# A two-layer diffusion backbone on one core: the MLP's down projection as seven products of quarter blocks instead of eight

## The chip, the cores and the metric

The kernel runs on one core of a Trainium2 chip. The metric is the time of one execution on the device in microseconds (us), from the first to the last instruction with what lies around them. TensorE (PE in the profile) multiplies matrices, VectorE (DVE) and ScalarE (ACT) work elementwise, GpSimd (POOL) does little here, and SyncE (SP) issues DMA transfers. Each engine works through its own list of instructions in a fixed order, and semaphores hold an instruction back until its inputs are there.

## The reference

Two layers over 512 latent tokens `x` and 256 context tokens `h`, width 1024, MLP width 4096, everything in float32. Cut to what matters:

```python
for l in range(2):
    last = l == 1
    sh1, sc1, g1, sh2, sc2, g2 = split(silu(c) @ w_ada[l] + b_ada[l])        # and the same of c_ctx
    ox, oc = token_mix(modulate(rmsnorm(x), sh1, sc1), modulate(rmsnorm(h), csh1, csc1), ...)
    x = x + g1 * ox
    x = x + g2 * (square(relu(modulate(rmsnorm(x), sh2, sc2) @ w_ff1[l])) @ w_ff2[l])
    if not last:
        h = h + cg1 * oc
        h = h + cg2 * (square(relu(modulate(rmsnorm(h), csh2, csc2) @ w_ff1[l])) @ w_ff2[l])
return rmsnorm(x, norm_final)
```

So layer 0 runs its MLP on 768 tokens and layer 1 on 512. `w_ff1` is 1024x4096 and `w_ff2` 4096x1024 in each layer.

## The kernel before

Features lie on the 128 partitions and tokens along the free axis. Float32 accuracy comes from split operands: every operand of a product is kept as a high part (a copy rounded to fp32r) and a low part (the rest), and a product of two blocks is three matmuls, high·high, high·low and low·high (`mm3`, recorded at L150). For a unit of weights (128x1024, 512 KB) SyncE loads the raw block, ACT writes the high part (`hi`, L158) and DVE subtracts it for the low part (`lo`, L167). Activations are split by the same two helpers.

`layer_ff` does the MLP in four chunks of 1024 hidden units. A chunk has two phases. FF1, the up projection: 8 tiles `A` of 128 units, each 8 blocks of `w_ff1` by all tokens (a 512-wide and, in layer 0, a 256-wide matmul for each of the three products). `evac` squares the rectified tile (ACT L1224, DVE L1225) and splits it into an `act` tile. FF2, the down projection: `residual_tasks` makes 8 tiles `res` of 128 outputs from the 8 `act` tiles, and `gate_update` (DVE L1137) adds each, times a gate, to the residual `x`.

In the last chunk the last two output tiles (`TAIL1`) take the token groups (0 to 255, 256 to 511, and in layer 0 512 to 767) one after the other, and the norm of one finished group is strewn among the tiles of the next: squares of `x` are summed (`stat_push`, L432), a product with ones (`ssum`) adds them over partitions, `rstd` (nv, nq, L442 to L446) makes the scale, and `norm_h` (hn at L459, h at L462 and L463) makes the split input of the next layer, whose first products are `rk`. At the very end `fin` (L498) scales the output instead.

`emit` walks the list of tasks in order and puts weight splits ahead of their use: 3 slots for split units (`N_W`), 2 for raw ones (`N_R`). The modulation vectors of layer 1 are not made by matmul but by DVE, as inner products of rows of `w_adaT` (`rows`, `dot`, L390), merged into layer 0's MLP as background work, with 3 slots for those rows. The last part of layer 0's own modulation is eight products on PE (`ada`) with rows of `w_ada` from the same 3 slots; they are merged into the first seven tasks of layer 0's MLP.

PSUM, where products land, has 8 banks of 512 float32 columns; the MLP uses three tiles of two banks and two of one.

## Time and profile before

| | us |
|---|---|
| median of 3 runs | 1603.75 (1602.11 to 1604.69) |
| profiled execution, span from first to last instruction | 1602.4 |
| PE busy in it | 1561.8 (97%) |
| DVE busy | 908.3 (57%) |
| ACT busy | 616.6 (38%) |

The profiled execution has the span of 1602.4 us; what lies around a span is not listed for it, and its span stands within the range of the three runs. A busy share of PE near 100% means that matmuls follow each other without a gap, and what another engine does then is hidden unless a matmul waits for it.

### The profile page before, as it was taken

Reading aid. Unit: us, or ns where it says so; the run is one execution under the profiler, and the core shown is the slowest. Engines: PE = TensorE matmul, PEld = TensorE weight load, DVE = VectorE, ACT = ScalarE, POOL = GpSimd, SP = SyncE. Lnnn points to the kernel's source line nnn. Section 1 sums busy time; section 2 is a strip of 40 time slices with the busy share of each in tenths; the row PEclk is TensorE's granted clock in tenths of the full one; section 3 lists DMA queues with packets and bytes.
Section 4 is the critical chain, followed back from the end, with each engine's and each line's share of the span. In section 5 each row is a group of like instructions: output and inputs, shape, how many; then the busy total and the mean of one; then the engine's idle time right before and its main releaser. Section 6 shows DMA issues by size and latency. Waiting matters only on the chain.

```text
span 1602.4 us, 22550 instructions
## 1 busy us (share of the span) xinstructions
PE 1561.8 (97%) x8884; PEld 1291.5 (81%) x8884; DVE 908.3 (57%) x1768; ACT 616.6 (38%) x1095; POOL 36.7 (2%) x75
## 2 busy tenths in 40 slices
PE   5999999999999999999999999999999999999997
PEld 2798667888888888888888899867878888888886
DVE  6565755886844454454545567686547434343344
ACT  5425567544531132122113234467654423232233
POOL 0110000000000000000000002001000000000000
PEclk9999999999999999999999999999999999999999
DMA  9352444553433333334444434334333333233332
GB/s 359 113 156 63 131 126 101 189 175 135 125 99 106 97 100 100 105 114 137 138 141 132 163 124 126 113 88 104 93 113 119 105 93 92 92 92 95 92 94 74
DMA packets 68009, 192.89 MB, mean 120 GB/s; under 512 B 8896, under 2 KB 11456, under 8 KB 67904
## 3 DMA queue, kind: packets, MB, share of 16 engines
q1 hardware_dynamic: 64512, 181.23, 36.4%
q0 software_dynamic: 2816, 9.70, 2.7%
q8 instruction: 70, 1.15, 0.3%
q10 hardware_dynamic: 576, 0.52, 0.1%
q14 instruction: 35, 0.29, 0.1%
HBM read 161.02 MB, written 10.49 MB: 107 GB/s over the span
## 4 chain that ended last, share of the span: by engine, by line
PE 93%; DVE 4%; ACT 2%; DMA 1%; issue 0%; SPq 0%; DVEq 0%; ACTq 0%
PE A L150 38%; PE res L150 30%; PE sc L150 4%; PE oe L150 4%; PE pv L150 3%; PE pT L925 3%; PE rv L150 2%; PE ada L150 2%; PE ro L150 1%; PE q L150 1%; DVE hn L459 1%; DMA raw<-w_ada 1%; PE rs L150 1%; DVE h L463 1%; PE v L150 1%
## 5 line engine op out<-in xcount | busy, mean ns | idle before, releaser
L150 PE MATMUL A<-h,wt 128*128 128x512 f32 (+1 forms) x3312 | 631.0, 350 | 4.8 <-ACT h L462 2.3
L150 PEld LDWEIGHTS A<-h,wt 128*128 128x128 f32 x3312 | 531.1, 190 | 102.7 <-DVE h L463 4.5
L150 PE MATMUL res<-act,wt 128*128 128x512 f32 (+1 forms) x2400 | 453.8, 351 | 0.0
L150 PEld LDWEIGHTS res<-act,wt 128*128 128x128 f32 x2400 | 386.4, 189 | 66.2
L158 ACT ACTIVATE wt<-raw 128x1024 fp32r<-128x1024 f32 (+1 forms) x176 | 185.8, 1057 | 385.2 <-PE res L150 327.1
L167 DVE TENSOR_TENSOR wt<-raw,wt 128x1024 fp32r<-128x1024 f32 (+1 forms) x176 | 215.2, 1223 | 48.5 <-ACT wt L158 48.3
L1137 DVE SCALAR_TENSOR_TENSOR x<-res,mod,x 128x512 f32<-128x512 f32 (+1 forms) x132 | 78.4, 618 | 244.8 <-PE res L150 239.9
L1225 DVE TENSOR_TENSOR ra<-ra,A 128x768 f32<-128x768 f32 (+1 forms) x64 | 52.5, 821 | 199.6 <-ACT ra L1224 199.6
L1224 ACT ACTIVATE ra<-A 128x768 f32<-128x768 f32 (+1 forms) x64 | 45.1, 705 | 285.6 <-PE A L150 285.6
L150 PE MATMUL sc<-k,q 96*128 96x512 f32 (+1 forms) x384 | 85.4, 351 | 2.0 <-ACT p L907 1.4
L390 DVE SCALAR_TENSOR_TENSOR rows<-rows,sbc 128x512 f32<-128x512 f32 x128 | 84.7, 686 | 3.9 <-DMA rows<-w_adaT 3.4
L150 PEld LDWEIGHTS sc<-k,q 96*128 96x128 f32 x384 | 62.9, 188 | 19.0 <-issue 5.9
L906 DVE TENSOR_REDUCE st<-sc 128x1 f32<-128x768 f32 x64 | 60.9, 953 | 21.6 <-PE sc L150 21.1
L926 ACT ACTIVATE pT<-pT 128x384 f32<-128x384 f32 x128 | 56.6, 493 | 41.9 <-PE pT L925 38.7
L150 PE MATMUL res<-mix,wt 128*128 128x256 f32 (+1 forms) x384 | 59.0, 313 | 2.3 <-DVE om L946 1.9
L907 ACT ACTIVATE p<-sc,st 128x768 f32<-128x768 f32 x64 | 58.0, 906 | 7.0 <-DVE st L906 5.8
L150 PE MATMUL oe<-mix,wt 128*128 128x512 f32 (+1 forms) x288 | 60.6, 362 | 0.0
L150 PEld LDWEIGHTS res<-mix,wt 128*128 128x128 f32 x384 | 53.0, 189 | 8.3 <-DVE om L946 2.8
L150 PEld LDWEIGHTS oe<-mix,wt 128*128 128x128 f32 x288 | 47.3, 188 | 10.4 <-issue 1.5
L925 PE MATMUL pT<-ident,p 128*128 128x128 f32 x384 | 53.5, 273 | 0.0
L167 DVE TENSOR_TENSOR act<-ra,act 128x768 fp32r<-128x768 f32 (+1 forms) x64 | 52.4, 818 | 0.0
L462 ACT ACTIVATE h<-hn,mod 128x256 fp32r<-128x256 f32 (+1 forms) x80 | 37.5, 522 | 37.0 <-DVE hn L459 37.0
(222 smaller groups left out, 1270.0 us busy)
## 6 DMA issues: line engine op xcount, KB each, us to landing
raw<-w_ff SPq DMA_DIRECT2D x128, 512.0 KB, 3.7
rows<-w_adaT SPq DMA_DIRECT2D x128, 256.0 KB, 3.5
raw<-w_in SPq DMA_DIRECT2D x22, 512.0 KB, 3.8
raw<-w_ada SPq DMA_DIRECT2D x16, 512.0 KB, 10.6
rows<-w_ada SPq DMA_DIRECT2D x32, 256.0 KB, 3.4
raw<-w_out SPq DMA_DIRECT2D x16, 512.0 KB, 3.8
x<-xd SPq DMA_DIRECT2D x8, 768.0 KB, 7.7
x<-xT SPq DMA_DIRECT2D x4, 768.0 KB, 7.0
```

The source lines that it names most:

```text
L150: self.nc.tensor.matmul(out, l, r, start=start, stop=stop)
L158: self.nc.scalar.activation(out, src, AF.Copy, **k)
L167: return self.nc.vector.tensor_tensor(out, src, hi.bitcast(F32), op=ALU.subtract)
L390: nc.vector.scalar_tensor_tensor(out, w, 1.0, self.sbc[:, v, half], op0=ALU.mult, op1=ALU.mult, accum_out=acc[:, v, i, j:j + 1])
L462: nc.scalar.activation(h[:, 0, o:o + n], t[:, :n], AF.Identity, bias=sh)
L906: nc.vector.tensor_reduce(st[:, 0:1], ps, axis=AX, op=ALU.max, negate=True)
L907: nc.scalar.activation(p, ps, AF.Exp, bias=st[:, 0:1], accum_out=st[:, 1:2])
L925: nc.tensor.transpose(ps[:, kt, :], p[:, (k0 + kt) * P:(k0 + kt + 1) * P], self.ident)
L926: nc.scalar.activation(s["pT", h, qt // 2][:, k0:k0 + 3, c], ps, AF.Copy)
L1137: self.gated = self.gated[-1:] + [self.nc.vector.scalar_tensor_tensor(x, ps[:, o:o + n], self.mod[l][:, chunk * 8 + k, cond:cond + 1], x, ...
L1224: nc.scalar.activation(t[:, 0, :w], ps[:, :w], AF.Relu)
L1225: nc.vector.tensor_tensor(t[:, 1, :w], t[:, 0, :w], ps[:, :w], op=ALU.mult)
```

## The change

In each chunk the down projection is a product of a weight matrix cut into 2x2 blocks (two halves of its outputs, two halves of its hidden units) with activations cut into 2x2 blocks (two halves of hidden units, two halves of tokens). Before, this is eight products of quarter blocks in all. Now it is seven (Strassen's scheme in Winograd's form), of sums and differences of blocks.

- Weights: quarters A11, A12, A22, A21 of `w_ff2` arrive as they are, 1 MB in two raw slots for a unit of kind "st"; DVE adds up S1 to S4 (`quarter`, L244). Seven pieces of 512 columns are then split for each unit (A21 is used in sums alone).
- Activations: for each pair of hidden tiles DVE forms T1 to T4 (`evac`, L1357 and L1369), and seven parts are split instead of four. The square is now made on ACT.
- Outputs: some of the seven products are gated into `x` at once (`gate`, L1418); others are collected over the chunks in `V` tiles named U, 5 and 7 (`keep`, L1357) and go into `x` at the end (`finish`). In the last chunk the tokens of the first half are finished first, then products S1 and S4 follow with the norm of the first half strewn among them.
- Tokens are in two halves: 384 and 384 in layer 0, 256 and 256 in layer 1. FF1 takes the same halves, and so do the norm and `rk` of layer 1.
- Layer 0 has eight chunks of 512 hidden units instead of four of 1024; layer 1 keeps four of 1024.
- All weights are split in pieces of 512 columns, with 6 slots for pieces and 4 raw ones, four pieces ahead. PSUM is eight single banks during the MLP.
- The `ada` products are merged into the first four entries of layer 0's list instead of seven; the modulation rows of layer 1 stop 40 entries before its end, not 36.

```diff
-N_W = 3
-N_R = 2
+N_W = 6
+N_R = 4
 RW = 512
-AS = 2
+OW = 576
+AP_ = 4
...
+    def quarter(self, u, i):
+        if i < 4:
+            return u.raw[i // 2][:, i % 2 * 512:i % 2 * 512 + 512]
+        if i not in u.sums:
+            a, b = {S1: (A21, A22), S2: (S1, A11), S3: (A11, A21), S4: (S2, A12)}[i]
+            a, b = self.quarter(u, a), self.quarter(u, b)
+            t = u.sums[i] = self.tmp("sum")[:, 0:512]
+            self.nc.vector.tensor_tensor(t, a, b, op=ALU.add)
+        return u.sums[i]
+    def split_piece(self, p):
+        u = p.unit
+        if u.kind == "st":
+            src, w = self.quarter(u, p.i), 512
+        else:
+            w = min(u.size, u.w - p.i * u.size)
+            src = u.raw[:, p.i * u.size:p.i * u.size + w]
+        p.t = self.wh.tile([P, 2, OW], F32R, tag="w", name=self.nm("wt"))
+        self.hi(p.t[:, 0, :w], src)
+        self.lo(p.t[:, 1, :w], src, p.t[:, 0, :w])
...
-        def evac(c, m, ps):
-            t = self.d("ra", F32)
-            nc.scalar.activation(t[:, 0, :w], ps[:, :w], AF.Relu)
-            nc.vector.tensor_tensor(t[:, 1, :w], t[:, 0, :w], ps[:, :w], op=ALU.mult)
-            f = act[c, m] = self.d("act")
-            self.hi(f[:, 0, :w], t[:, 1, :w])
-            self.mark = self.lo(f[:, 1, :w], t[:, 1, :w], f[:, 0, :w])
-
+        def evac(c, m, half, parts):
+            p, odd = divmod(m, 2)
+            if half == 0:
+                st["b", odd] = self.tmp("b")
+            b = st["b", odd]
+            o = half * hw
+            for ps, at, n in parts:
+                nc.scalar.activation(b[:, at:at + n], ps, AF.Relu)
+            nc.scalar.activation(b[:, o:o + hw], b[:, o:o + hw], AF.Square)
+            h1, h2 = b[:, 0:hw], b[:, hw:w]
+            neg = lambda x, y, z: nc.vector.scalar_tensor_tensor(x, y, -1.0, z, op0=ALU.mult, op1=ALU.subtract)
+            if half == 0:
+                put(c, p, B21 if odd else B11, h1)
+                return
+            if not odd:
+                t = st["t"] = self.tmp("T")
+                add(t[:, 0:hw], h1, h2, ALU.subtract)
+                put(c, p, T1, t[:, 0:hw])
+                return
+            t, v = st["t"], self.tmp("T")
+            put(c, p, B22, h2)
+            add(v[:, 0:hw], h2, st["b", 0][:, hw:w], ALU.subtract)
+            put(c, p, T3, v[:, 0:hw])
+            neg(t[:, hw:w], t[:, 0:hw], h2)
+            put(c, p, T2, t[:, hw:w])
+            neg(v[:, hw:w], t[:, hw:w], h1)
+            put(c, p, T4, v[:, hw:w])
...
+        def gate(m, half, ps, neg=False):
+            g = self.ng[:, m] if neg else self.mod[l][:, 40 + m]
+            o = half * hw
+            self.mark = None
+            for at, n, cond in halves[half]:
+                x = self.X(m)[:, at:at + n]
+                self.mark = nc.vector.scalar_tensor_tensor(x, ps[:, at - o:at - o + n], g[:, cond:cond + 1], x,
+                                                           op0=ALU.mult, op1=ALU.add)
+            self.gated = self.gated[-1:] + [self.mark]
...
+        def keep(c, j, name, ps):
+            v = st[name][j]
+            if c == 0 and (name, j) not in st:
+                st[name, j] = True
+                nc.scalar.activation(v, ps, AF.Copy)
+            else:
+                self.mark = add(v, v, ps)
+        use = {A11: (B11, lambda c, j, ps: (keep(c, j, "U", ps), gate(2 * j, 0, ps))),
+               S1: (T1, lambda c, j, ps: keep(c, j, "5", ps)),
+               A12: (B21, lambda c, j, ps: gate(2 * j, 0, ps)),
+               S4: (B22, lambda c, j, ps: gate(2 * j, 1, ps)),
+               S3: (T3, lambda c, j, ps: keep(c, j, "7", ps)),
+               S2: (T2, lambda c, j, ps: keep(c, j, "U", ps)),
+               A22: (T4, lambda c, j, ps: gate(2 * j + 1, 0, ps, True))}
+        def both(c, j, ps):
+            gate(2 * j, 1, ps)
+            gate(2 * j + 1, 1, ps, True)
+        def product(c, u, i, j, name, then=None):
+            q, f = use[name]
+            ps = self.B([P, hw], "f2")
+            t = u.pieces[name].t
+            for p in range(CP):
+                s = slice((i * CP + p) * P, (i * CP + p + 1) * P)
+                self.mm3(ps, t[:, 0, s], t[:, 1, s], *part(c, p, q), p == 0, p == CP - 1)
+            (then or f)(c, j, ps)
+        def block(c, blk, u, names, fs={}):
+            cost = 3 * CP * hw / 2.2
+            return [Task(cost, lambda i=i, n=n: product(c, u, i, MP * blk + i, n, fs.get(n)), (u.pieces[n],))
+                    for n in names for i in range(MP)]
+        def finish(j):
+            U, v5, v7 = (st[n][j] for n in "U57")
+            add(v7, v7, U)
+            gate(2 * j + 1, 0, v7, True)
+            add(U, U, v5)
+            add(v7, v7, v5)
+            gate(2 * j, 1, U)
+            gate(2 * j + 1, 1, v7, True)
+        def push(j, half):
+            for m in (2 * j, 2 * j + 1):
+                self.stat_push(m, half * hw, hw)
...
-            for m in range(m0, 8):
-                out.append(self.lin_task(u1[m], H, gs, lambda ps, c=c, m=m: evac(c, m, ps)))
-            end = c == N_CHUNK - 1
-            out += self.residual_tasks(l, u2, lambda k, c=c: act[c, k], NK, 5, whole, groups,
-                                       TAIL1 if end else 0, then if end else None)
+                out.append(Task(2 * self.lin_cost(NK, [(0, hw)] * 2), lambda us=us: up_two(us[:2]), tuple(us[:2])))
+            blocks = [Unit(a["w_ff2"][l, c * n_blk + blk], 2048, "st") for blk in range(n_blk)]
+            n = n_blk if c < n_chunk - 1 else n_blk - 2
+            if n < n_blk:
+                out.append(Task(0, self.stat_start))
+            for blk in range(n):
+                out += block(c, blk, blocks[blk], (A11, S1, A12, S4, S3, S2, A22))
+                if n < n_blk:
+                    out.append(Task(0, lambda j=blk: (finish(j), push(j, 0), push(j, 1))))
+        c = n_chunk - 1
+        js = [range(MP * blk, MP * blk + MP) for blk in range(n_blk)]
+        for blk in range(n, n_blk):
+            out += block(c, blk, blocks[blk], (A11, A12, S3, S2, A22))
+            out.append(Task(0, lambda blk=blk: (blocks[blk].sums.clear(), [(finish(j), push(j, 0)) for j in js[blk]])))
+        rest = []
+        for blk in range(n, n_blk):
+            rest += block(c, blk, blocks[blk], (S1, S4), {S1: both})
+            rest.append(Task(0, lambda blk=blk: [push(j, 1) for j in js[blk]]))
+        late = list(then[0])
+        for i, t in enumerate(rest):
+            out.append(t)
+            share = -(-len(late) // (len(rest) - i))
+            out += late[:share]
+            late = late[share:]
+        return out + list(then[1])
...
-            tasks += e.pop(("mid", l), []) + merge(ff[:7], e.pop(("ff1", l), [])) + merge(ff[7:FT], e.pop(("ff", l), [])) + ff[FT:]
+            tasks += e.pop(("mid", l), []) + merge(ff[:4], e.pop(("ff1", l), [])) + merge(ff[4:FT], e.pop(("ff", l), [])) + ff[FT:]
```

**DVE in a down projection of layer 0.** In the middle of a chunk DVE's list before is this (`wt` is the low part of a whole weight unit, `x` a gate update, `rows` and `dot` the background inner products):

```order
L1137 SCALAR_TENSOR_TENSOR x_701_3700<-res_6104,mod_157,x_701_3700 128x512
L1137 SCALAR_TENSOR_TENSOR x_701_3700<-res_6104,mod_157,x_701_3700 128x256
L390 SCALAR_TENSOR_TENSOR dot_6155,acc_6093<-rows_5969,sbc 128x512
L167 TENSOR_TENSOR wt_6228<-raw_6160,wt_6228 128x1024
L390 SCALAR_TENSOR_TENSOR rows_5969,acc_6093<-rows_5969,sbc 128x512
L1137 SCALAR_TENSOR_TENSOR x_701_3700<-res_6165,mod_157,x_701_3700 128x512
L1137 SCALAR_TENSOR_TENSOR x_701_3700<-res_6165,mod_157,x_701_3700 128x256
```

and with the change (`f` is a product's PSUM tile, `ng` the negated gate):

```order
L217 TENSOR_TENSOR wt_8732<-sum_8730,wt_8732 128x512
L217 TENSOR_TENSOR wt_8751<-raw_8388,wt_8751 128x512
L1357 TENSOR_TENSOR V_4299<-V_4299,f_1565_8754 128x384
L468 SCALAR_TENSOR_TENSOR rows_8695,acc_8633<-rows_8695,sbc 128x512
L1357 TENSOR_TENSOR V_4299<-V_4299,f_1567_8765 128x384
L244 TENSOR_TENSOR sum_8773<-sum_8730,raw_8388 128x512
L1418 SCALAR_TENSOR_TENSOR x_729_3779<-f_1571_8780,ng_4727,x_729_3779 128x384
L244 TENSOR_TENSOR sum_8775<-sum_8773,raw_8388 128x512
L1418 SCALAR_TENSOR_TENSOR x_730_3780<-f_1572_8788,ng_4727,x_730_3780 128x384
L244 TENSOR_TENSOR sum_8796<-raw_8388,raw_8389 128x512
L217 TENSOR_TENSOR wt_8777<-sum_8775,wt_8777 128x512
L1357 TENSOR_TENSOR V_4299<-V_4299,f_1575_8801 128x384
```

Sums of quarters and additions into `V` now stand between the weight splits, in one list with them.

**DVE between the layers.** Before, the last tiles of layer 0 and the norm of tokens 0 to 255 follow each other like this (the gate update of `res_8419` is for the next token group):

```order
L1137 SCALAR_TENSOR_TENSOR x_702_3701<-res_8357,mod_157,x_702_3701 128x256
L432 TENSOR_TENSOR ss_7954<-ss_7954,sq_8383 128x256
L1137 SCALAR_TENSOR_TENSOR x_702_3701<-res_8391,mod_157,x_702_3701 128x256
L1137 SCALAR_TENSOR_TENSOR x_702_3701<-res_8419,mod_157,x_702_3701 128x256
L432 TENSOR_TENSOR ss_7954<-ss_7954,sq_8445 128x256
L442 TENSOR_SCALAR nv_8459<-ssum_8456 128x256
L445 SCALAR_TENSOR_TENSOR nq_8460<-nv_8459,nq_8460 128x256
```

With the change, the rows ahead of the first half's norm are the ends of `finish` and gates of the second half (mixed halves take two instructions, since context tokens have gates of their own):

```order
L1357 TENSOR_TENSOR V_4299<-V_4299,V_4300 128x384
L1357 TENSOR_TENSOR V_4301<-V_4301,V_4300 128x384
L1418 SCALAR_TENSOR_TENSOR x_730_3780<-V_4299,mod_155,x_730_3780 128x128
L1418 SCALAR_TENSOR_TENSOR x_730_3780<-V_4299,mod_155,x_730_3780 128x256
...
L1418 SCALAR_TENSOR_TENSOR x_730_3780<-f_1712_9596,mod_155,x_730_3780 128x128
L1418 SCALAR_TENSOR_TENSOR x_730_3780<-f_1712_9596,mod_155,x_730_3780 128x256
L1418 SCALAR_TENSOR_TENSOR x_730_3780<-f_1712_9596,ng_4727,x_730_3780 128x128
L1418 SCALAR_TENSOR_TENSOR x_730_3780<-f_1712_9596,ng_4727,x_730_3780 128x256
L528 TENSOR_SCALAR nv_9610<-ssum_9607 128x384
L217 TENSOR_TENSOR wt_9618<-raw_9482,wt_9618 128x512
L531 SCALAR_TENSOR_TENSOR nq_9611<-nv_9610,nq_9611 128x384
```

From the first product of this last down projection to the last `h` of the first half DVE's list has 144 rows.

**PE at the start of layer 0's MLP.** Behind the first pair of up tiles, PE's list with the change goes on with two `ada` products, and the next up tile stands behind them (a row's waits are given in brackets):

```order
L200 MATMUL f_842_4329<-h_769_4030,wt_4181 128x256 x3
L200 MATMUL f_840_4327<-h_770_4031,wt_3935 128x256 [waits Activation_49]
L200 MATMUL f_840_4327<-h_770_4031,wt_3935 128x256 [waits DVE_49]
L200 MATMUL f_840_4327<-h_770_4031,wt_3935 128x256
L200 MATMUL f_842_4329<-h_770_4031,wt_4181 128x256 x3
L200 MATMUL ada_4308<-rows_4313,sc 32x512 [waits DMAHW5_49]
L200 MATMUL ada_4308<-rows_4318,sc 32x512 [waits DMAHW6_49]
L200 MATMUL f_866_4549<-h_763_4024,wt_4320 128x384 x3
```

Two of the eight `ada` products stand ahead of the pair, these two right behind it, and the other four within the next two up tiles; before, they were spread over six up tiles.

## Rows read from the trace of the kernel before

**Rows 1.** The page: busy time by engine, granted clock, chain by engine.

```profile
PE 1561.8 (97%) x8884; PEld 1291.5 (81%) x8884; DVE 908.3 (57%) x1768; ACT 616.6 (38%) x1095; POOL 36.7 (2%) x75
...
PEclk9999999999999999999999999999999999999999
...
PE 93%; DVE 4%; ACT 2%; DMA 1%; issue 0%; SPq 0%; DVEq 0%; ACTq 0%
```

**Rows 2.** Stretches: us, then PE, PEld, DVE, ACT, POOL busy (instructions), clock, DMA.

```profile
477.00:545.00 68.00, 68.00 (x387) 59.23 (x386) 30.48 (x65) 10.09 (x11) 0.00 (x0) 1.00 0.32 97
545.00:613.00 68.00, 68.00 (x386) 59.27 (x385) 36.55 (x68) 19.41 (x23) 0.00 (x0) 1.00 0.34 101
...
1276.00:1321.00 45.00, 45.00 (x194) 36.17 (x193) 16.21 (x18) 9.54 (x11) 0.00 (x0) 1.00 0.34 95
...
1588.00:1602.00 14.00, 4.82 (x33) 3.91 (x31) 9.39 (x25) 4.14 (x10) 0.00 (x0) 0.81 0.45 150
```

**Rows 3.** The chain that ended last: start, length, engine, group, line, instructions.

```profile
477.06 67.84 PE res L150 x384
...
884.10 59.44 PE res L150 x360
...
955.11 5.90 PE A L150 x48
...
974.02 11.49 PE A L150 x48
...
1275.94 44.98 PE res L150 x192
...
1545.83 42.20 PE res L150 x216
1597.14 2.01 DVE fin L498 x6
```

**Rows 4.** DVE by line and shape: busy, mean ns; idle before.

```profile
L167 DVE TENSOR_TENSOR wt<-raw,wt 128x1024 fp32r<-128x1024 f32 x170 | 207.9, 1223 | 44.3 <-ACT wt L158 44.1
...
L1137 DVE SCALAR_TENSOR_TENSOR x<-res,mod,x 128x512 f32<-128x512 f32 x68 | 51.0, 750 | 235.6 <-PE res L150 230.7 <-DMA x<-xd 4.9
...
L1137 DVE SCALAR_TENSOR_TENSOR x<-res,mod,x 128x256 f32<-128x256 f32 x64 | 30.3, 477 | 9.2 <-PE res L150 9.2
```

**Rows 5.** DVE's timeline between the layers: start, duration, line, instructions.

```profile
949.55 1.27 DVE L459 SCALAR_TENSOR_TENSOR hn<-x,G,ss 128x256 f32<-128x256 f32 x3
950.73 1.27 DVE L463 SCALAR_TENSOR_TENSOR h<-hn,mod,h 128x256 fp32r<-128x256 f32 x3
...
953.91 0.42 DVE L432 TENSOR_TENSOR ss<-ss,sq 128x256 f32<-128x256 f32 x1
954.24 0.42 DVE L442 TENSOR_SCALAR nv<-ssum 128x256 f32<-128x256 f32 x1
...
954.97 1.22 DVE L167 TENSOR_TENSOR wt<-raw,wt 128x1024 fp32r<-128x1024 f32 x1
956.10 0.42 DVE L445 SCALAR_TENSOR_TENSOR nq<-nv,nq 128x256 f32<-128x256 f32 x1
```

**Rows 6.** DVE's timeline at the start of layer 0's MLP.

```profile
423.83 0.69 DVE L390 SCALAR_TENSOR_TENSOR dot<-rows,sbc 128x512 f32<-128x512 f32 x1
...
424.44 0.95 DVE L1225 TENSOR_TENSOR ra<-ra,A 128x768 f32<-128x768 f32 x1
425.31 0.69 DVE L390 SCALAR_TENSOR_TENSOR rows<-rows,sbc 128x512 f32<-128x512 f32 x1
...
441.49 0.69 DVE L390 SCALAR_TENSOR_TENSOR dot<-rows,sbc 128x512 f32<-128x512 f32 x1 [4.14 <-DMA rows<-w_adaT]
```

**Rows 7.** DMA issues of the page: KB each, us to landing.

```profile
rows<-w_ada SPq DMA_DIRECT2D x32, 256.0 KB, 3.4
```

**Rows 8.** DVE's timeline at the end of the program.

```profile
1594.57 0.43 DVE L442 TENSOR_SCALAR nv<-ssum 128x256 f32<-128x256 f32 x1
```

322 lines of the change are left out of this document (211 added, 111 removed).

## The prediction

> **What bounds the kernel now.** I read the page first: PE is busy for 97% of the span at the full clock, DVE for 57%, and the chain that ended last runs over PE for 93% [rows 1]. The table of stretches says the same for the MLP: PE is busy in all of each phase, while DVE has work for 30.5 of 68 us in a down projection of layer 0, 36.6 of 68 in an up projection and 16.2 of 45 in a down projection of layer 1 [rows 2]. So before, every DVE instruction there is hidden, and time goes with matmuls. The two places where the chain leaves PE are the joints behind the last down projections: between the layers, from 955.11 to 974.02, PE has `rk` to do as the norm's groups come, and at the end DVE has the final norm [rows 3].
>
> **The gain on PE.** The price of a matmul is read from the chain: 192 pairs of a 512 and a 256 wide one take 67.84 us, 353.3 ns a pair, and 192 of 512 columns take 44.98 us, 234.3 ns each [rows 3]. The 256 wide one costs 119.0 ns beside the wide one; half of 234.3 would be 117.2. Between these, 384 columns are 175.7 to 176.7 ns; I take 176. A half chunk of layer 0 is 7 products x 4 output pairs x 2 blocks x 3 = 168 matmuls, 29.6 us where 33.9 us (half of 67.84) stood. A chunk of layer 1 is 336 of 256 columns, 39.4 us (40.0 at 119.0) where 44.98 stood. Over all chunks this is 8 x 4.3 = 34.8 us and 4 x 5.6 = 22.3 us, 57 us together if nothing else waits. Up projections keep their columns and their time.
>
> The rule that would speak against this is in the Trainium skill, page TensorE: Matmul & The Clock Gate, section Back-to-back issue gap: in a stream of weight loads and matmuls it puts 128 columns at about 81 ns and 512 at about 131, so that a narrow matmul costs far more than its share. By it 256 columns would be an estimated 98 ns, and layer 1 would lose some 31 us by trading 768 matmuls of 512 for 1344 of 256. The trace disagrees: 119.0 against 234.3 ns is half [rows 3].
>
> **The price on DVE.** Durations overlap, so I take starts. An addition of 256 columns starts 0.33 us before the next instruction, one of 1024 columns 1.13 [rows 5]; on that line 384 columns are 0.47 us and 512 are 0.60, and 768 would be 0.87, which rows 6 show. An inner product of 512 columns takes 0.61 [rows 6]. An update with a scalar for each partition takes 0.393 at 256 columns [rows 5]; a gate of 512 lasts 750 ns and one of 256 lasts 477 [rows 4], less the 0.09 us by which durations exceed starts [rows 5], so 384 columns are 0.53 and 128 are 0.26.
>
> A half chunk of layer 0 then asks of DVE, in its down projection: 14 low parts (8.4 us), 8 sums of quarters (4.8), 16 additions into `V` (7.5), 12 gates of 384 and 4 split ones (9.0), and about 10 inner products (6.1): 36 us beside 29.6 of PE. In its up projection: 8 low parts (4.8), 14 low parts of activations (6.6), 8 combinations (3.8) and 6 inner products (3.7): 19 beside 33.9. On the whole DVE has 55 of 63.5 us and keeps up, but not in the down projection, where it falls back by 6.4 us. It also starts late, by the tail of the last hidden pair (relu and square on ACT, then about 3.5 us of combinations and their low parts), which makes a lag of some 10 us. The cover is the four pieces that are split ahead: each feeds 12 matmuls, 2.1 us, 8.4 in all. What is left, about 2 us, PE waits for low parts of the last pieces, in each of the seven half chunks that are followed by another. Low end 0 (the order of DVE's rows puts splits ahead of gates often enough), high end 6 (the banks that wait for gates hold PE too). So a half chunk is 31.6 us, a gain of 2.3, not 4.3.
>
> **Between the layers.** From the first product of the last down projection to the last `h` of the first half, DVE's list has 144 rows, and nothing of layer 1 can start on PE before them: 24 additions of `V` (11.3 us), 36 gates (16 of 384, 20 of 128 and 20 of 256 in pairs: 21.6), 14 low parts of weights (8.5), 7 sums (4.2), 7 inner products (4.3), 12 sums of squares (5.6), norm of the first half (9.9), tail of the hidden pair (1.9): 67.5 us with the small ones. PE has 29.6 us of products to put beside it. In front stand about 4 us until DVE gets there, behind it about 2.5 for the statistics product and ACT's part of the scale, 12.0 for the norm of the second half (its split columns make 32 instructions and the scale) and 1 for the last matmuls of `rk`, whose first half hides beside that norm: 87 us from the start of the last down projection to `rq0`. Before, 884.10 to 974.02 is 89.9 us [rows 3], but for a whole chunk of 67.84. Layer 0 from its first down projection on, up projections left out: before 3 x 67.84 + 89.9 = 293.4; after 7 x 31.6 + 87 = 308.2. That is **+15 us**, with -14 and +28 for the stall's ends, and about 4 us either way for the joint.
>
> **Start of layer 0's MLP.** The `ada` products now follow within two up tiles of the first pair; their rows come 3.4 us after issue [rows 7], through three slots shared with the rows of the inner products, for which DVE itself already waits 4.14 us once [rows 6]. Two rounds that PE waits for instead of working make **+6** (0 if the rows are issued while the pair runs, 10 with a third round). What hid them before was three more up tiles.
>
> **Layer 1.** There are no inner products here, and DVE has 28 low parts (16.9), 12 sums (7.2), 16 additions (5.4) and 16 gates (6.3) in a down projection, 35.9 us beside 39.4. Three chunks gain 45.0 - 39.4 - 0.4 = 5.2 each, **-15.6**. In the last chunk the sums are formed twice for two blocks, and `finish` and squares come on top: 26 additions, 26 gates, 24 low parts, 14 sums and 9 sums of squares are 45.0 us before the last products' gates. With 4 in front and 7.5 for those gates, the squares and the first `fin`, the last `nv` stands at 56.5 us from the chunk's start. From `nv` to the end is 1602.4 - 1594.57 = 7.8 us [rows 8], in all 64.3. Before, 1545.83 to 1602.4 is 56.6 [rows 3]. **+8**.
>
> **Sum.** 15 + 6 - 15.6 + 8 = +13 us on the profiled execution's span of 1602.4, so 1615.4; the median of the runs shown stands 1.35 above that span: **1617 us**. Of the 57 us that PE saves, 35 return at the joint between the layers (87 - 29.6 against 89.9 - 67.8), 14 as stalls of the half chunks, 13 at the end, 6 at the start and 1 in layer 1. Finer pieces elsewhere I cost at nothing: the same columns are split, and in attention DVE's list is not what PE waits for in the chain; without that cover, 0.07 us for each further instruction.
>
> **Rivals.**
> - *DVE is hidden.* The eight banks and the pieces ahead absorb the lag, no half chunk stalls, and `ada` rows are in time: 13 - 14 - 6 = -7, 1597 us; with the joints hidden as well it is the whole 57 us, 1547. For it speaks that DVE's load over a chunk is below PE's; against it the 144 rows, which stand in a fixed order ahead of `rk`. This is the other side, and it decides when the stall is below about 1 us a half chunk and the `ada` rows are in time. Chance 0.32, most of it between 1575 and 1600.
> - *Nothing to measure.* Stalls near 1 us and a start at +3 give +3 or less. Chance 0.1 for within 0.2%, about 3.2 us, which is what a measurement of this kernel can tell from no change.
> - *DVE bounds all of layer 0.* Stalls of 6 us and ten from `ada`: +45, 1649. Gates late in the list hold banks, and up projections can't start. It needs DVE's lag not to be worked off in the up projection, where it has 15 us to spare. Chance 0.08.
> - *The clock falls at the joint.* PE idles for some 40 of the 87 us between the layers. In the last 14 us of the trace PE is busy for 4.8 and the granted clock is 0.81 [rows 2], so part of that stretch ran at the lower of the two levels, 1.2 GHz. At that level `rk` and the 48 matmuls that took 11.49 us at 974.02 [rows 3] would take twice their time: about +12 on the forecast, 1629. The Trainium skill says so too (same page, section Part 1: The HAM clock gate): an array that idles goes to half its clock. Chance 0.1.
>
> **How the numbers follow.** The forecast's own case has 0.4: +5 to +25, 1608 to 1628. Slower together 0.4 + 0.08 + 0.1 = 0.58, same 0.1, faster 0.32. The range leaves out 0.1 at each end: the whole gain and the better half of the hidden case below, a bound DVE above: 1572 to 1640.
>
> **What would show it.** Matmuls of 384 columns at 175 to 177 ns and 256 at 117 to 119; in the stretches of down projections of layer 0 DVE busy above 95% and PE gaps of 1 to 3 us ahead of products, released by a low part (L217); a gap of PE of 30 to 45 us in pieces between the layers, released by `x` and `h` on DVE; waits of PE for rows of `w_ada` behind the first pair; layer 1's first three down projections without gaps. The prediction is wrong if PE stays busy for 97%, or if the last product of layer 0 and `rq0` are less than 25 us apart, or if the stalls are released by DMA of raw units, whose new slots I cost at nothing.

## The result and the profile after

The changed kernel takes 1645.04 us (median of 4 runs, 1641.43 to 1647.41) against 1602.93 for the kernel before beside it: a ratio of 1.0269, 95% interval 1.0257 to 1.0282. It is slower, as forecast, but by about 40 us where 13 us were forecast.

The page of the changed kernel: its span, the busy row, the row of the granted clock in 40 slices, and the chain that ended last by engine.

```profile
span 1642.0 us, 26299 instructions
PE 1533.6 (93%) x9840; PEld 1375.8 (84%) x9840; DVE 1245.5 (76%) x2761; ACT 830.4 (51%) x1746; POOL 38.0 (2%) x78
PEclk8999999999899999999999968999999999999997
PE 76%; DVE 18%; ACT 2%; DMA 2%; issue 1%; SPq 0%; DVEq 0%; ACTq 0%
```

Against [rows 1], PE fell from 97 to 93% busy, DVE rose from 57 to 76%, and the chain leaves PE for DVE in 18% of the span. The dips of the clock row show where: the start of layer 0's MLP, the joint between the layers, and the end.

The same in stretches (columns: stretch, its length, busy time of PE, weight loads, DVE, ACT and POOL with counts, granted clock, DMA share, GB/s). In order: start of layer 0's MLP, a down projection of a half chunk, the last half chunk's products, norm and `rk` behind it, a down projection of layer 1, its last one, the end.

```profile
404.00:420.00 16.00, 7.10 (x25) 3.79 (x24) 15.82 (x40) 8.97 (x22) 0.00 (x0) 0.70 0.22 74
524.00:557.00 33.00, 31.44 (x173) 29.22 (x172) 31.36 (x70) 11.54 (x21) 0.00 (x0) 1.00 0.29 95
917.00:989.00 72.00, 37.50 (x174) 34.56 (x173) 69.41 (x157) 25.23 (x48) 0.00 (x0) 0.75 0.28 100
989.00:1012.00 23.00, 21.70 (x100) 19.76 (x98) 14.09 (x39) 10.09 (x22) 0.00 (x0) 0.82 0.12 37
1317.00:1357.00 40.00, 40.00 (x340) 40.00 (x340) 36.20 (x69) 23.09 (x48) 0.00 (x0) 1.00 0.39 122
1573.00:1623.00 50.00, 41.18 (x303) 38.95 (x302) 48.52 (x108) 25.51 (x54) 0.00 (x0) 0.92 0.13 43
1623.00:1642.00 19.00, 9.18 (x44) 8.15 (x44) 11.51 (x31) 5.88 (x14) 0.00 (x0) 0.68 0.34 111
```

In [rows 2] PE was busy for all of every such phase of the MLP; of the rows shown here that holds for layer 1's down projection alone. From 917 to 989 DVE is busy for 69.4 of 72 us and PE for half of it. In the down projection of the second row, PE stands twice (PE's timeline: start, busy time, line, operation, and in brackets the idle time before it and what ended that):

```profile
546.63 7.57 PE L200 MATMUL f<-act,wt 128*128 128x384 f32 x36 [0.90 <-ACT wt L208]
554.70 2.33 PE L200 MATMUL f<-act,wt 128*128 128x384 f32 x12 [0.50 <-DVE x L1418]
```

The first wait ends on ACT's high part of a piece, the second on a gate that frees a PSUM bank. From start to start the gaps are 1.24 and 0.84 us, where 0.17 is usual; the idle time listed is shorter because the ends of matmuls are modelled.

Reading the trace stage by stage (starts of the first and last matmul of each stage) gives this ledger, in us against the kernel before. The joint is the time from the first product of layer 0's last down projection to `rq0`.

| Term | forecast | measured |
|---|---|---|
| up to the first product of layer 0's output projection | 0 | +2.7 |
| from there to layer 0's first down projection | +6 | +14.7 |
| seven half chunks with a successor | -16.1 | -18.2 |
| joint between the layers | 87 long, +31 | 95.4 long, +39.3 |
| layer 1 up to its first MLP product | 0 | +2.8 |
| layer 1's MLP | -7.6 | -1.5 |
| sum, before rounding | +13 | +39.6 |

Two of the misses are read directly. First the PE timeline at the start of layer 0's MLP:

```profile
404.28 0.88 PE L200 MATMUL res<-mix,wt 128*128 128x256 f32 x6
411.41 1.22 PE L200 MATMUL ssum<-ss,one 128*128 128x256 f32 x2 [6.25 <-DVE ss L518]
413.50 1.22 PE L200 MATMUL ssum<-sq,one 128*128 128x256 f32 x2 [0.87 <-ACT sq L514]
416.50 1.92 PE L200 MATMUL ada<-rows,sc 128*32 128x512 f32 x4 [1.78 <-DVE nv L528]
418.36 1.86 PE L200 MATMUL f<-h,wt 128*128 128x256 f32 x7
```

The first product `f` of the MLP starts at 418.36; before, its counterpart `A` started at 402.43 and ran while the third token group was still normed. `f` takes the first group only, whose `h` had been ready. What it now stands behind is `nv`, the read of the last `ssum` out of PSUM: `begin` closes the old PSUM pools and opens eight single banks, and the first tile of a new pool waits for the last reader of all that lay there. I call this the layout wait.

Then the chain of waits at the joint and at the end of the changed kernel (start, length, engine and piece):

```profile
985.65 0.60 DVE wt L217
988.39 2.91 PE ssum L200 x4
991.33 0.59 ACT ss L527
991.94 0.57 DVE nv L528
992.55 18.89 PE A L200 x93
...
1012.39 2.83 PE A L200 x11
...
1621.74 0.79 DVE x L1418 x2
1622.92 2.07 PE ssum L200 x4
1625.00 4.65 PE f L200 x24
1631.61 0.67 DVE fin L592 x2
1632.67 1.14 PE ssum L200 x4
1636.93 2.01 DVE fin L592 x6
```

The `rk` products (tile `A` at 992.55) take both halves; the last `h` of the first half was done by 989.29, but they begin only behind `nv`, the statistics of the second half, and `rq0` follows 19.8 us later. At the end, the last `f` products stand behind `ssum` in PE's order.

### The profile page after: what moved, and what is told of

Same layout as the page of the kernel before. It is cut to its first block, busy times and chain, and to the rows that moved or that the text cites. A ratio compares the mean times of both kernels' runs of the same rounds, so it can differ in the third digit from the quotient of the medians.

```text
span 1642.0 us, 26299 instructions
## 1 busy us (share of the span) xinstructions
PE 1533.6 (93%) x9840; PEld 1375.8 (84%) x9840; DVE 1245.5 (76%) x2761; ACT 830.4 (51%) x1746; POOL 38.0 (2%) x78
## 4 chain that ended last, share of the span: by engine, by line
PE 76%; DVE 18%; ACT 2%; DMA 2%; issue 1%; SPq 0%; DVEq 0%; ACTq 0%
PE f L200 40%; PE A L200 10%; PE sc L200 4%; DVE x L1418 3%; PE oe L200 3%; DVE wt L217 3%; PE pv L200 3%; PE res L200 3%; DVE V L1357 3%; PE pT L1025 2%; PE rv L200 2%; DVE sum L244 2%; PE ada L200 2%; DVE rows L468 1%; PE ro L200 1%
## 5 line engine op out<-in xcount | busy, mean ns | idle before, releaser
L200 PEld LDWEIGHTS f<-h,wt 128*128 128x128 f32 x3120 | 451.6, 190 | 5.6 <-issue 3.8
L200 PE MATMUL f<-h,wt 128*128 128x256 f32 (+1 forms) x3120 | 454.1, 308 | 1.2 <-DVE nv L528 1.0
L200 PE MATMUL f<-act,wt 128*128 128x384 f32 (+1 forms) x2688 | 419.7, 316 | 19.7 <-DVE x L1418 10.4
L200 PEld LDWEIGHTS f<-act,wt 128*128 128x128 f32 x2688 | 401.6, 193 | 35.9 <-ACT wt L208 12.8
L217 DVE TENSOR_TENSOR wt<-raw,wt 128x512 fp32r<-128x512 f32 (+1 forms) x320 | 218.8, 689 | 88.1 <-ACT wt L208 85.6
L208 ACT ACTIVATE wt<-raw 128x512 fp32r<-128x512 f32 (+1 forms) x320 | 195.0, 626 | 165.4 <-PE f L200 64.0
L200 PE MATMUL A<-h,wt 128*128 128x512 f32 (+2 forms) x864 | 172.5, 358 | 1.8 <-DVE nv L528 1.3
L200 PEld LDWEIGHTS A<-h,wt 128*128 128x128 f32 x864 | 144.4, 192 | 28.3 <-DVE nv L528 2.4
L217 DVE TENSOR_TENSOR wt<-sum,wt 128x512 fp32r<-128x512 f32 x128 | 86.8, 689 | 12.0 <-ACT wt L208 10.7
L1418 DVE SCALAR_TENSOR_TENSOR x<-f,mod,x 128x256 f32<-128x256 f32 (+2 forms) x186 | 88.5, 501 | 1.4 <-PE f L200 1.0
L1357 DVE TENSOR_TENSOR V<-V,f 128x384 f32<-128x384 f32 (+1 forms) x162 | 79.3, 511 | 0.1
L217 DVE TENSOR_TENSOR act<-b,act 128x384 fp32r<-128x384 f32 (+1 forms) x96 | 46.8, 489 | 42.8 <-ACT act L208 42.7
L1006 DVE TENSOR_REDUCE st<-sc 128x1 f32<-128x768 f32 x64 | 60.7, 953 | 15.6 <-PE sc L200 15.2
L217 DVE TENSOR_TENSOR act<-T,act 128x384 fp32r<-128x384 f32 (+1 forms) x128 | 60.5, 487 | 12.4 <-ACT act L208 11.4
L1026 ACT ACTIVATE pT<-pT 128x384 f32<-128x384 f32 x128 | 56.5, 491 | 22.9 <-PE pT L1025 22.4
```

What stands on the lines that cost most here:

```text
L200: self.nc.tensor.matmul(out, l, r, start=start, stop=stop)
L208: self.nc.scalar.activation(out, src, AF.Copy, **k)
L217: return self.nc.vector.tensor_tensor(out, src, hi.bitcast(F32), op=ALU.subtract)
L1006: nc.vector.tensor_reduce(st[:, 0:1], ps, axis=AX, op=ALU.max, negate=True)
L1026: nc.scalar.activation(s["pT", h, qt // 2][:, k0:k0 + 3, c], ps, AF.Copy)
L1357: add = lambda x, y, z, op=ALU.add: nc.vector.tensor_tensor(x, y, z, op=op)
```

## The experiments

**1. The layout wait alone.** Two-bank tiles of the old layout are kept and handed out half by half, so nothing is closed at the MLP's start.

```diff
+    def bank(self, w):
+        if not self.bq:
+            self.bi += 1
+            if self.bi % 4:
+                t = self.A("f", (P, 2, 512))
+                self.bq = [t[:, 0, :], t[:, 1, :]]
+            else:
+                self.bq = [None, None]
+        t = self.bq.pop(0)
+        return (self.B([P, 512], "f") if t is None else t)[:, :w]
-            self.psum(0, 8)
+            self.bq, self.bi = [], 0
-                ps = self.B([P, hw], "f1")
+                ps = self.bank(hw)
```

> The changed kernel, but the MLP keeps the PSUM layout of the stages around it (three tiles of two banks, two of one) and hands their halves out as eight banks, in place of laying PSUM out anew at the start of each MLP and again ahead of layer 1's first products. Theory A (the new layout is a barrier: the first up products wait until the last statistics of the norm ahead have been read, and rk of the first half waits for the statistics of the second): PE's first up product starts some 10 us earlier at layer 0's MLP, 2 to 3 earlier at layer 1's, and rk of the first half runs beside the norm of the second, 7 us: about 1622 on the span of 1642.0. Rival B (what is late there is the norm itself or the rows of w_ada): no change beyond 3 us, 1639 to 1645. Two halves of a tile are freed together, which may cost up to 5 us in the down projections under either.

Measured: 1678.06 us, ratio 1.0463 (1.0436 to 1.049). The wait is indeed gone: the first `f` starts at 405.93. The first down projection ends (its last matmul starts, here and below) at 486.01 instead of 490.91, with 14 matmuls of the next up projection among its own. But a half chunk now takes some 71 us for 65.4: between 500 and 900 us `f` products in down projections wait 30.1 us, half of it for gates (`x`), against 7.2 between 480 and 920 in the changed kernel. Two tiles that share a pair of banks come free together here; run 5, with single banks, is back at 65.5 us. So the wait was shown, and this remedy cost more than it gave.

**2. Eight products in the last chunk of each layer.** U, 5 and 7 are finished during the last up projection, and the last products go straight into the gates.

```diff
+            if c == n_chunk - 1:
+                put(c, p, B22 if odd else T1, h2)
+                return
...
+                if c == n_chunk - 1 and (m + 1) % (CP // 2) == 0:
+                    out.append(Task(0, lambda j=(m + 1) // (CP // 2) - 1: finish(j)))
...
-            out += block(c, blk, blocks[blk], (A11, A12, S3, S2, A22))
+            out += plains(c, blk, blocks[blk], (0, 1))
```

> The changed kernel with the last chunk of each layer as eight products instead of seven: no sums of quarters and no additions into V there, and finish is done in that chunk's up projection. Theory A (DVE's list of 144 rows, 67.5 us, sets the joint between the layers, and its 45 us the end): DVE's list from the first gate to the last h of the first half is 29.5 us, below PE's 33.8; the joint from the last down projection to rq0 falls from 95.4 to 50 to 54 us, the end from 68.9 to 57 to 59: 1588 on the span of 1642.0, plus up to 5 where finish makes DVE late in the last up projection. Rival B (the joint is set by the chain of statistics, scale, first products and the low clock, not by the amount of DVE's work): the joint stays above 80 us and the time above 1625.

Measured: 1605.8 us, ratio 1.0024 (1.0013 to 1.0035). The joint shrank from 95.4 to 64.7 us (923.10 to 987.83), the end from 68.9 to 57.1. With eight products in the two last chunks, 4 of the 42 us that the change loses are left. The expectation was 18 us too low, 11 to 15 of it at the joint, where PE still stands from 957.50 to 968.05 until the second half's `nv`.

**3. Both edits together.**

> Both edits together: no new PSUM layout, and the last chunk as eight products. Theory A: the barrier at the starts of the MLPs is gone as well, 12 us, and the joint gains 2 to 4 from rk beside the norm: 1588 - 15 = 1573 on the span, below the kernel before by about 30. Rival B, under which the first two edits give little: above 1620. If the coarser banks stall the down projections: 1578 to 1585.

Measured: 1639.36 us, ratio 1.0236 (1.0219 to 1.0253), far above the 1573 expected: the half chunks were as long as in run 1. Eight products in the last chunks gain 39 us on run 1, as much as run 2 gained on the changed kernel.

**4. Without the quarter sums.** A raw quarter stands in for each S1 to S4, so the outputs are not the reference's.

```diff
+        if i >= 4:
+            return self.quarter(u, {S1: A21, S2: A22, S3: A11, S4: A12}[i])
```

> The changed kernel with the sums of weight quarters left out (a raw quarter stands in the place of S1 to S4), so that part of the computation is missing; 128 additions of 0.60 us less on DVE, everything else the same. Theory A (DVE's amount of work makes the stalls in layer 0's down projections, 1 to 3 us in each, and sets joint and end): stalls gone, -12 us; joint -4 (7 sums), end -8 (14 sums): 1618. Rival B (the stalls come from PSUM banks or from ACT's high parts, whose count is the same): under 8 us in all, 1634 or more.

Measured: 1603.31 us, ratio 1.0017 (0.9999 to 1.0036), span 1599.8. Every down projection of a half chunk but the last is 28.95 us without a gap (the first 29.04; 31.7 on the mean with the sums); the joint is 89.2 and the end 56.1. So the sums, 0.6 us each on DVE, cost 42 us where I had expected 24: 7 x 2.8 in the half chunks, 6 at the joint, 12.8 at the end, and 2.8 in layer 1's first three chunks, whose stages all ran at the quicker of two speeds (last section). The edit takes away DVE's additions and, with them, ACT's wait for their results ahead of the high parts; this run alone does not say which of the two held PE. Run 7 bears on that. Row of a down projection of this kernel, with no idle PE:

```profile
512.00:545.00 33.00, 33.00 (x192) 33.00 (x191) 27.65 (x65) 14.72 (x27) 0.00 (x0) 1.00 0.25 77
```

**5. One PSUM layout from the output projection through `rk`.** Six single banks and two more are opened once; `res` and `rk` take two single banks each, and the `ada` products follow behind the first pair.

```diff
-        out.append(Task(0, lambda: self.psum(3, 2)))
+        out.append(Task(0, lambda: self.psum(0, 2, 6)))
-            ps = self.A("res")
+            ps = Banks(self.C, "res")
-            self.psum(0, 8)
+            self.bi = -1
-            tasks += e.pop(("mid", l), []) + merge(ff[:4], e.pop(("ff1", l), [])) + merge(ff[4:FT], e.pop(("ff", l), [])) + ff[FT:]
+            tasks += e.pop(("mid", l), []) + ff[:2] + merge(ff[2:4], e.pop(("ff1", l), [])) + merge(ff[4:FT], e.pop(("ff", l), [])) + ff[FT:]
```

> The changed kernel with PSUM kept in one layout from the output projection of a layer to the end of rk of the next (one pool of six single banks, one of two for statistics and a part of the products), so that no new layout stands at the start of an MLP or ahead of rk, and the ada products behind the first pair of up tiles. Theory A (the layout is the barrier, and the first attempt lost by tying banks in pairs, which cost 5 us a half chunk): first up product at 406 where 418.4 stood, 8 to 10 us there, 6 to 7 from rk beside the norm's second half, 5 to 8 at the start of layer 1's MLP: 1617 to 1623 on the span of 1642.0. Rival B (eight free banks are what keeps the down projections near their time, and any split of them costs): the half chunks are longer by 1 us or more each, 1630 to 1640. Rival C (PE is held there by the norm, not by the layout): 1640 or more.

Measured: 1626.89 us, ratio 1.0151 (1.0133 to 1.017). The windows of the joint in this kernel, from the last half chunk's start at 918.83 to `rq0` at 1007.89:

```profile
919.00:991.00 72.00, 51.43 (x224) 42.56 (x223) 69.78 (x159) 25.65 (x50) 0.00 (x0) 0.83 0.32 105
991.00:1008.00 17.00, 12.45 (x51) 10.61 (x50) 14.21 (x38) 10.40 (x25) 0.00 (x0) 0.80 0.09 28
```

PE does 50 matmuls more in the first window than the changed kernel from 917 to 989; 48 are the first half of `rk`, from 972.30 on. The joint is 89.1 us, the 7.5 us wait ahead of layer 1's MLP is gone (1257.68 to 1257.98 instead of 1262.30 to 1269.81), and the end is 65.4. At the start of layer 0 the first `f` comes at 405.28, and yet the first down projection ends at 492.19, no earlier: there PE waits 3.6 us for the rows of `ada` and 2.9 for ACT's copy of their product instead.

**6. Runs 2 and 5 together.**

> The same layout, and the last chunk of each layer as eight products with finish in its up projection (the second experiment, 1606.4 span). Theory A: the gains add up, since rk there waited from 957.5 to 968.05 for the second half's statistics: 1606.4 - 9 - 7 - 7 = 1583, range 1578 to 1590. Rival B: 1596 or more.

Measured: 1594.98 us, ratio 0.9952 (0.9936 to 0.9969): the first version that beats the kernel before. The joint is 60.6 us. It missed its expectation by some 10 us: 3 at the joint, where 4.2 were gained and not 7, and 7 at the start of layer 0, where the first down projection ends only 2.2 us earlier than in run 2. The chain waits for rows there twice and then for ACT and `adaT`:

```profile
447.42 2.59 DMA rows<-w_ada
450.05 1.06 PE ada L223 x2
451.13 2.57 DMA rows<-w_ada
453.74 1.04 PE ada L223 x2
454.79 5.95 PE f L223 x24
```

**7. The quarter sums on GpSimd instead of DVE.**

```diff
-            self.nc.vector.tensor_tensor(t, a, b, op=ALU.add)
+            self.nc.gpsimd.tensor_tensor(t, a, b, op=ALU.add)
```

> The changed kernel with the sums of weight quarters on POOL instead of DVE. If it is DVE's work that the sums cost (theory A), the time goes most of the way to that of the kernel without sums (1599.8 span): 1600 to 1612. POOL does nothing else then, and 8 sums in 65 us leave it room up to some 5 us each. Rival B: POOL's additions and DVE's instructions hold each other up (DVE's additions of 384 columns last over 0.60 us where they last 0.56), or a chain of three sums on POOL comes too late for S4: above 1625, and above 1642 if a sum takes over 3 us.

Measured: 1643.73 us, ratio 1.0258 (1.0243 to 1.0273), no gain at all. The stretch from 484 to 930 us, all the half chunks from the first one's end on, in the changed kernel:

```profile
484.00:930.00 446.00, 438.63 (x2470) 425.75 (x2469) 382.32 (x863) 189.08 (x359) 0.00 (x0) 1.00 0.36 116
```

and in this one:

```profile
484.00:930.00 446.00, 433.52 (x2458) 426.92 (x2457) 394.23 (x803) 192.93 (x361) 81.61 (x55) 1.00 0.36 115
```

DVE has 60 instructions less and is busy for 12 us more. Its groups of that stretch (line, engine, operation, forms, count, busy time, mean ns of one, idle time before them), first in the changed kernel:

```profile
L468 DVE SCALAR_TENSOR_TENSOR rows<-rows,sbc 128x512 f32<-128x512 f32 x91 | 61.3, 688 | 0.1
L1357 DVE TENSOR_TENSOR V<-V,f 128x384 f32<-128x384 f32 x103 | 54.3, 553 | 0.0
L217 DVE TENSOR_TENSOR act<-T,act 128x384 fp32r<-128x384 f32 x56 | 29.9, 554 | 4.9 <-ACT act L208 4.7
```

then here:

```profile
L468 DVE SCALAR_TENSOR_TENSOR rows<-rows,sbc 128x512 f32<-128x512 f32 x89 | 66.9, 765 | 0.3
L1357 DVE TENSOR_TENSOR V<-V,f 128x384 f32<-128x384 f32 x101 | 52.5, 541 | 0.0
L217 DVE TENSOR_TENSOR act<-T,act 128x384 fp32r<-128x384 f32 x56 | 45.1, 827 | 6.6 <-ACT act L208 6.5
```

Groups with both inputs in SBUF became longer (554 to 827 ns for `act`, 688 to 765 for `rows`); those that read one input from PSUM (`V`, with `f`) did not. What matters is whether a sum runs on GpSimd at the same time: 25 of these `act` overlap one and take 1169 ns on the mean, the other 31 take 552; six `V` overlap one and take 541. And a sum lasts twice as long on GpSimd as on DVE (0.69 us), over the whole of this kernel:

```profile
L244 POOL TENSOR_TENSOR sum<-sum,raw 128x512 f32<-128x512 f32 x66 | 101.0, 1530 | 147.3 <-issue 69.2 <-DVE T L1369 43.6 <-DVE ss L518 8.2
```

The Trainium skill has this rule: page SBUF — State Buffer, section Who interferes with whom, says that a DVE instruction with two SBUF inputs contends with a GpSimd instruction that reads SBUF, and one with at most one SBUF input doesn't. The rows agree on both counts. Its page GPSIMD Engine Reference, section 3.1, gives an addition of 2048 elements 1.96 times DVE's time; here, with 512, it is 1530 to 688, 2.2 times, contention in it.

The other half of rival B, that the chain of sums on GpSimd comes too late, is out for the half chunks. From 484 to 920 us ACT waits 93.5 us for DVE's sums in the changed kernel and never for GpSimd's in this one. PE still waits, and each time for DVE (who waited for whom, us in total, times, longest):

```profile
PE f L200 <- DVE x L1418: 6.9, 6, 2.5
PE f L200 <- DVE V L1357: 3.0, 5, 1.3
PE f L200 <- DVE wt L217: 2.5, 2, 1.3
```

So in this run it is the length of DVE's list that holds PE, and that is the likelier reading of run 4 too.

**8. Run 6 with the sums on GpSimd.**

> All three: one PSUM layout, last chunks as eight products, sums on POOL. Theory A: 1583 less the stalls of seven half chunks, 2.8 us each: 1563, range 1558 to 1572, which is 2.4% below the kernel before. Rival B, where POOL's sums hold up DVE: 1590 or more.

Measured: 1596.06 us, ratio 0.9964 (0.9951 to 0.9976), equal to run 6 within the intervals. I put the missing gain down to what run 7 shows; it was not tested apart here.

**9. Eight products in every chunk**, with the chunks, pieces and PSUM layout of the change.

```diff
+            if True:
+                put(c, p, B22 if odd else T1, h2)
+                return
...
-                out += block(c, blk, blocks[blk], (A11, S1, A12, S4, S3, S2, A22))
+                out += plains(c, blk, blocks[blk], (0, 1))
```

> All chunks of both layers take eight products again; the chunks of 512 units, the pieces, the PSUM layout and the half chunks stay as the change has them. It is run 2 with the seven products taken from the other chunks too. Theory A (seven products pay where the half chunk or chunk still ends with TensorE): in layer 0 a stage of 192 matmuls of 173.3 ns with its step is 33.4 us against the 32.2 that run 2 showed with seven products and their stall, +1.2 in seven half chunks, +8; in layer 1 45.4 against 39.75 in three chunks, +17, less about 0.5 in each of four up projections. That is +23 on run 2: span 1629, no gap longer than 0.5 us in a half chunk. Rival B (the sums and the seven parts on VectorE, not the products' count, are what the change costs and gains nothing anywhere): the time of run 2 or less, 1600 to 1606.

**10. Run 9 with the one layout of run 5.**

> Run 9 with the one PSUM layout of run 5: eight products everywhere, chunks of 512 units, pieces. It stands to run 6 as run 9 to run 2. Theory A: +23 on run 6, span 1616, so still slower than before by about 1% with the layout mended, and the whole gain of seven products is the 23 us between the two. Rival B: equal to run 6, 1593, and the layout and the chunks alone beat the kernel before.

**11. Run 6 with eight products in all of layer 0**, seven in the first three chunks of layer 1.

> Run 6 with eight products in all of layer 0 and seven in the first three chunks of layer 1 alone. Theory A (seven products are worth 1.2 us in a half chunk of layer 0, since VectorE takes back the rest): +6 to +10 on run 6, span 1601, about the kernel before. Rival C (the sums of layer 0 cost more elsewhere, at the start of the MLP and under the joint, than they gain in its half chunks): equal to run 6 or up to 8 below it, 1585 to 1593.

Measured: run 9 1624.17 us, ratio 1.0147 (1.013 to 1.0164); run 10 1605.59, 1.002 (1.0008 to 1.0032); run 11 1587.41, 0.9913 (0.9899 to 0.9928). Seven products gain: run 9 stands 18 us above run 2, run 10 about 11 above run 6, where 23 were expected of both. Run 10 is no faster than the kernel before, so chunks, pieces and the one layout by themselves gain nothing.

Runs 9 and 10 also show the layout wait with little else in the way, since DVE has no sums and no seven parts to do. From the end of the output projection to the end of the first down projection, in run 9 and then in run 10:

```profile
405.00:492.00 87.00, 77.36 (x463) 70.83 (x462) 59.34 (x148) 30.84 (x67) 0.00 (x0) 0.92 0.35 115
403.00:480.00 77.00, 76.50 (x460) 69.62 (x460) 58.81 (x150) 30.47 (x68) 0.00 (x0) 1.00 0.40 130
```

With the one layout, and the `ada` products behind the first pair, this stretch is 9.8 us shorter, the joint 3.9 (60.5 instead of 64.4) and the way from `rq0` to the last product of layer 1's first up projection 6.4.

But in layer 0 they cost on balance: run 11 is 7.6 us below run 6. The rows of run 6 and then of run 11 for the first half chunk's down projection and what stands ahead of it:

```profile
440.00:482.00 42.00, 35.15 (x152) 28.39 (x152) 29.06 (x75) 14.15 (x30) 0.00 (x0) 0.88 0.36 115
```

```profile
440.00:482.00 42.00, 42.00 (x235) 39.23 (x234) 25.95 (x69) 9.04 (x16) 0.00 (x0) 1.00 0.42 134
```

Without the seven parts and the sums, PE has no idle time in this stretch; over the whole start it waits 0.5 us for `ada` rows in run 11 and 3.9 in run 6. That down projection ends at 492.36 in run 6 and at 482.03 in run 11; from there to the last half chunk's start run 6 is 4.3 us quicker. Rival C of that expectation holds, with its cost in one place.

**12. Seven products in the middle of layer 0**: run 6 with eight also in layer 0's first half chunk.

```diff
+        eight = lambda c: c == n_chunk - 1 or c == 0 and not last
-            if c == n_chunk - 1:
+            if eight(c):
                 put(c, p, B22 if odd else T1, h2)
```

> Run 11 with seven products again in half chunks 2 to 7 of layer 0, eight in its first and last. Run 6 and run 11 differ by 10.3 us in the first half chunk of layer 0 (end of its down projection 492.36 and 482.03, against run 11 and with the adaLN rows waiting) and by 4.3 us the other way from there to the last half chunk's start. Theory A (the loss of seven products in layer 0 is all in the first half chunk, where the adaLN rows wait behind the sums on VectorE): 4.3 us below run 11, span 1582.5, median about 1583. Rival B (the rows and sums only wait in the next half chunk instead, and the stall comes there): equal to run 11, 1587, or up to 3 us above it.

Measured: 1575.0 us, ratio 0.9843 (0.9828 to 0.9858), the best version, 1.6% below the kernel before. Its page:

```profile
span 1572.6 us, 26242 instructions
PE 1521.4 (97%) x9936; PEld 1368.3 (87%) x9936; DVE 1166.0 (74%) x2591; ACT 806.4 (51%) x1700; POOL 38.0 (2%) x78
PEclk9999999999999999999999999999999999999999
PE 85%; DVE 10%; DMA 3%; ACT 2%; issue 1%; SPq 0%; DVEq 0%; ACTq 0%
```

PE is as busy as in [rows 1] with 40 us less to do. Of the 14.2 us between the spans of runs 11 and 12, layer 0's half chunks give 8.7: their six down projections together are 9.9 us shorter than eight products would be. That is twice the 4.3 us of the expectation. Another 2.7 lie ahead of the MLP and 3.7 in layer 1, neither of which the edit touches: the first is within the scatter between these programs, the second is in the last section. The last 1 us goes the other way. So theory A holds in direction, and part of the size is luck.

## Why the prediction was right in sign and short in size

In one sentence: the step that failed is that the forecast had no term for the new PSUM layout, behind which products wait that the sum took as hidden, above all the first half of `rk`; runs 5, 9 and 10 show that wait. Of the 26 us between forecast and measurement, 8 to 9 lie at the start of layer 0's MLP, 8 at the joint, 6 in layer 1's MLP, 5 to 6 in stages put at nothing; the half chunks gave 2 more than forecast.

- **The gain on PE** was right. Matmuls of 384 columns go at 173.3 ns (forecast 176, from bounds 175.7 to 176.7, so a little outside them), those of 256 at 117.3 to 118.7 (117 to 119). Up projections in layer 0 became quicker for it, 33.1 us; those of layer 1 0.6 us slower, 45.57 against 44.98 from start to start, which I had at no change.
- **A half chunk of 31.6 us** measured 31.72 for its down projection, on the mean of seven. The loss in it was 2.8, not 2, on a shorter stage: 2.6 to 3.4 in six of them, while the first has no wait and loses 1.7 at a granted clock of 0.94 (460 to 491 us). Its cause was right, DVE's list falls behind: without the sums the stall is gone (run 4), with them on GpSimd DVE is no less busy and it stays (run 7). The sign "released by a low part (L217)" was not: PE's waits end on ACT's high parts, for which ACT had waited for DVE's sums, and on gates. The rival *DVE bounds all of layer 0* is out, and so is *DVE is hidden*.
- **The joint** is the larger miss at one place. DVE's list was right: from 920.21 to 989.29 it took 69.1 us, forecast 67.5, and the last `h` of the second half ends at 1004.9, 15.6 us on (forecast 14.5). The step that failed is the next one, `rk`, "whose first half hides beside that norm": 1 us of `rk` was to be left then, and 7.5 were. It was behind the layout wait, which the prediction had nowhere. Run 5, without it, has 89.1 us for the forecast 87. The rival *The clock falls at the joint* was right as a mechanism but small: granted 0.75 and 0.82 in the windows above, between the levels of 2.4 and 1.2 GHz, so in part at the lower one; the starts of `rk`'s 96 matmuls span 19.1 us there against 95 x 173.3 ns = 16.5, +2.6 where that rival had 12.
- **Start of layer 0's MLP**, "two rounds that PE waits", +6: this did not happen in the changed kernel, where PE never waits there for rows of `w_ada`. Between the last up product and the first of the down projection 4.6 us go to `ada`, to a wait of 2.3 for ACT's copy of its product, and to `adaT`; the layout wait stood ahead of that with some 10 more, and the third token group no longer had PE work beside its norm. The waits for rows that the prediction meant do come where the layout wait is gone: 3.6 us in run 5, 3.9 in run 6.
- **Layer 1.** The three chunks measured 39.7 (forecast 39.4). In the last one DVE's list took 45.7 (forecast 45.0), but "the last `nv` stands at 56.5 us" failed: it stood at 61.3, since the last 36 products come behind `ssum` in PE's order; these 4.8 us are the end's whole excess (68.9 for the forecast 64.3). In run 5 all products stand ahead of that `ssum` (1611.85), and the end is 65.4; what in the layout moved them there was not isolated.
- **Finer pieces elsewhere at nothing**: +2.7 ahead of the output projection and +2.8 between the joint and layer 1's MLP. The second contains a wait of 7.5 ahead of the MLP that run 5 removes. The cause of the first stays open: the output projection starts at 368.31 instead of 365.65, and in the experiments anywhere from 366.2 to 370.1.

So the one thing left out, the layout wait, is worth about 10 at the start (runs 9 and 10), 4 to 6 at the joint and 6 to 7 ahead of layer 1's MLP in the places where it stands. Taking it out of the changed kernel does not give the sum of these, because the rows of `ada` then take its place at the start: run 5 gave 18 on the median, 14.6 on the span, some 3.6 of that at the end of the program. The sizes of DVE's lists were right within 3%, so its account of DVE's work was sound; its account of what stands in front of PE was not. What the prediction priced as fixed, eager work on DVE at the joint and end, could be left out: eight products in three of the twelve chunks, with the one PSUM layout, turn +2.7% into -1.6%.

## What to carry to other kernels

A scheme that trades matmuls for elementwise work belongs in stages where another chunk's matmuls lie behind to absorb the lag, and not in a first stage where weights and side inputs compete for the same engine, nor in the last, where its tail is the path. (Layer 1's first chunk has no side inputs and kept seven products without a wait.) When an edit re-partitions PSUM between stages, list the last reader of every old tile: the first tile of the new layout waits for the last of them, whatever its own inputs. And before work is moved off VectorE to GpSimd, look at whether what stays reads both inputs from SBUF.

## What the runs showed that I had not expected

- A matmul of 384 columns goes at 173.3 ns, 0.451 ns a column; the pair of 512 and 256 before took 353.3, 0.460 [rows 3]. Equal widths were 2% better than the mixed pair.
- Moving 60 sums from DVE to GpSimd raised DVE's busy time from 382 to 394 us in one stretch (run 7).
- Stages of 384 matmuls of 256 columns take 44.94 us in some kernels (runs 4, 9, 10, 12) and 45.45 in others (the changed one, runs 2, 5, 6, 8, 11), and in run 7 both. All of them are at a granted clock near 1.00. Stages of 336 go with them, 39.31 or 39.75. Why is open; it is worth about 3.7 us over layer 1.
- Why the half chunks of run 12 stall less than those of run 6 (29.1 to 32.3 us of down projection against 31.9 to 32.8) with the same work in them is open too.
